# Single weight jobs of the mixers and the second block written as one 512-column and one 256-column matmul per k tile

## The chip, the cores and the metric

The kernel runs on one core of one Trainium2 chip. The metric is the device time of one execution in microseconds (us), as the median of several runs. The core has a matrix engine (PE, or TensorE, with its weight loads shown apart as PEld), two engines for elementwise work (ACT, or ScalarE, and DVE, or VectorE), a slower third (POOL, or GpSimd) and SP, which here only issues DMA transfers. Each engine works through its own instructions in a fixed order; they wait for one another by semaphores.

## What is computed

The reference is two stacked models on a sequence of 256 positions of width 2048, in fp32. The first has two layers, each of four mixers on one projection and a gated feed-forward part (5632 wide):

```python
for l in range(DEPTH):
    u = rms_norm(h, norm_pre_mix[l])
    p = (u @ w_in[l]).astype(jnp.float32)
    p_ret, p_hgrn, p_ml, p_rw = split_cols(p, GROUP_COLS)
    o_ret = retention_group(p_ret)
    o_hgrn = hgrn2_group(p_hgrn, lower_bounds[l], hgrn_norm_w[l])
    o_ml = mlstm_group(p_ml, ...)
    o_rw, v_first = rwkv7_group(p_rw, ...)
    mixed = jnp.concatenate([o_ret, o_hgrn, o_ml, o_rw], axis=-1) @ w_out[l]
    h = h + rms_norm(mixed, norm_post_mix[l])
    u = rms_norm(h, norm_pre_ffn[l])
    ffn = (jax.nn.silu(u @ w_ffn_gate[l]) * (u @ w_ffn_up[l])) @ w_ffn_down[l]
    h = h + rms_norm(ffn, norm_post_ffn[l])
```

The second ("block 2") is one layer of sparse attention and dilated attention on another such projection, merged and added to its input.

## The kernel before

**How a product is made.** All large products are weight streams: 512 KB of weights at a time come by a DMA of SP into a `raw` buffer (3 of them); `prep` (line 97) splits them into a high part `hi` (ACT's CAST, L108) and a low part `lo` (DVE's subtraction, L112), with 4 buffers of each; PE multiplies them with the activations, which are kept split in the same way, side by side in one tile of 512 columns: `x_hi` in columns 0 to 255, `x_lo` in 256 to 511. A product of fp32 accuracy is the sum hi·x_hi + hi·x_lo + lo·x_hi.

**Two kinds of streams.** `stream_a` (line 115) makes a block of 128 outputs, transposed, from 16 k tiles of 128 inputs, with the weights loaded into PE (128x128) and the activations streamed. A job is a tuple (weights, what to do at the end, a flag). With the flag True, a k tile takes three matmuls of 256 columns, all into the left half of a PSUM bank (L174 hi·x_hi, L175 hi·x_lo, L176 lo·x_hi): a *triple*. With False it takes one matmul of 512 columns, whose two halves are hi·x_hi and hi·x_lo (L178), and one of 256 columns for lo·x_hi into the left half (L179): a *pair*, and the two halves of the bank must be added afterwards. `half_sum` (L271) does so: ACT copies the right half out (L274), DVE adds the left half (L276). The feed-forward part and the merge at the end of block 2 use pairs, the mixers and block 2's other jobs triples. `stream_b` (line 213) makes 256x512 outputs with the activations loaded and the weights streamed, three 512-column matmuls to a step (L225, L226, L227), in two banks.

**Banks.** Streams take their banks from a pool of two (`sbank`, named `s` in the trace); the small products of the mixers use six others (`g`). A job of `stream_a` holds one `s` bank until its last reader is done, so the next job runs in the other; a `stream_b` takes both.

**The mixers.** `mixers` writes the code of a layer in a mixed order: 38 single jobs (`job_a`, L1342 is DVE's multiplication by the norm's factor at the job's end; `run_a`, `need`/`mix_job` call it) and 6 `run_b` of `stream_b`, and between them the small work of the four mixers, hundreds of matmuls of 32 to 128 columns with steps on ACT, DVE and POOL. The last third of a layer's mixers goes: RWKV7's output (`rw_out`, L1199 to L1234), the gates of mLSTM (`ml_gates`, L755 to L777), its values by `run_b(2)` (drained by ACT at L1512 into a tile `v`, with a memset of POOL ahead), then mLSTM's pairs. `v` and the gate tiles lie in memory that RWKV7's pool has given back, so the first to write them waits for the last steps of `rw_out`.

**Order.** The program is written with a scheduler that runs ahead of time: it estimates each instruction's duration, and within the priorities that the code sets (`K.first`, `issue_after`) fixes the order of each engine. So the order of the rows is a result, not written by hand, and another mix of instructions gives another order.

**Block 2.** 24 single jobs (`job`, L1888 is the ACT copy at a job's end) stand between the attention's work; 8 further jobs (those whose activations are `u`, with the flag 2) keep their triples in both kernels.

Of the kernel before, what the change touches and what calls it, by code (L numbers as in the profile page):

```python
# [13 lines left out]
OP = mybir.AluOpType  # L14
# [24 lines left out]
class Core:  # L39
# [228 lines left out]
            side = sides[i]  # L268
            self.stream_b(ws[i], orders[i] if orders else range(nk), lhs, done, None if side is None else [self.g(side), self.g(side)], i == 3, beside)

    def half_sum(self, bank):  # L271

        e0 = self.t(self.ev, [128, 256], "e0", 2)
        self.nc.scalar.copy(e0, bank[:, 256:512])  # L274
        e1 = self.t(self.ev, [128, 256], "e1", 2)
        self.nc.vector.tensor_tensor(e1, bank[:, 0:256], e0, op=OP.add)  # L276
        return e1

# [1046 lines left out]
def mixers(K, l, A, entry, dram, V):  # L1325

    nc, tc = K.nc, K.tc
    feed, late, rs, load = entry
    wa, wb = A[f"wina{l}"], A[f"winb{l}"]
    place = {n: i for i, n in enumerate(JOBS)}  # L1330
    outer, left, right = ExitStack(), ExitStack(), ExitStack()

    def pool(name, side, cx):
        return cx.enter_context(tc.tile_pool(name=f"{name}{l}", bufs=1, side=side, reuse_waits="tile"))

    def job_a(name, make):

        cell = []

        def done(bank):  # L1340
            dst, view = make()
            nc.vector.tensor_tensor(view, bank, rs(), op=OP.mult)  # L1342
            cell.append(dst)
        return (wa[place[name]], done, True), cell

    def run_a(name, make):
        job, cell = job_a(name, make)
        K.stream_a([job], K.uk, FULL)
        return cell[0]
# [7 lines left out]
    def padded(G, n, bufs=2):  # L1357
        def make():
            x = G.t([128, 256 + n], "x", bufs)
            nc.gpsimd.memset(x[:, 0:n], 0.0)  # L1360
            return x, x[:, n:256 + n]
        return make
# [12 lines left out]
    op = pool("o", "left", outer)  # L1375
# [8 lines left out]
    def mixed(x, i, name, bufs=1):  # L1384
        return R.shifted(x, w["mu"][:, i:i + 1], name, bufs)
# [7 lines left out]
    def mix_job(name):  # L1393
        (wt, done, _), cell = job_a(name, padded(R, 1))

        def both(bank):
            done(bank)
            i, to, bufs = where[name]
            got[name] = mixed(cell[0], i, to, bufs)
        return (wt, both, True)  # L1400

    def need(*names):
        for n in names:
            if n not in got:
                K.stream_a([mix_job(n)], K.uk, FULL, bank=K.g() if len(got) == 6 else None)
        return [got[n] for n in names]

    def begin(ph):
        load(ph)
        if ph[0] == 4:  # L1410
            w.update(columns(K, l, A))

    K.stream_a([mix_job(n) for n in HEADS], K.uk, FIRST if l else START, feed, late, load and begin, wa[0:4])
    rs.nat()
    w["wua"] = wua
# [57 lines left out]
    op = pool("o0", "right", right)  # L1473
# [26 lines left out]
    op = pool("o2", "left", left)  # L1500
# [110 lines left out]
class Ada:  # L1611
# [7 lines left out]
    def done(self):  # L1619

        K, nc = self.K, self.K.nc
        vec = K.t(K.base, [128, 80], "vec2")
        with K.tc.issue_after(K.last_hi.ins):
            nc.scalar.dma_start(vec, self.A["vec2"])
        nc.vector.tensor_tensor(self.cols, self.cols, vec[:, 0:48], op=OP.add)
        self.shift = self.cols[:, 0:16]
        self.scl = K.t(K.base, [128, 16], "scl")
        nc.vector.scalar_tensor_tensor(self.scl, self.cols[:, 16:32], 1.0, vec[:, 48:64], op0=OP.add, op1=OP.mult)
        self.post = K.t(K.base, [128, 16], "post")
        nc.vector.tensor_tensor(self.post, self.cols[:, 32:48], vec[:, 64:80], op=OP.mult)  # L1630
        self.kvb = K.t(K.base, [128, 8], "kvb")
        self.zero = K.t(K.base, [128, KT], "zero")
        nc.vector.memset(self.zero, 0.0)
# [193 lines left out]
def block2(K, A, mo, ada, prow):  # L1827

    nc, tc = K.nc, K.tc
    G = Groups(K, None, 2)  # L1830
    T = Attn(K, A)
    ja, jb = iter(range(200)), iter(range(10))
    wa, wb = A["win2a"], A["win2b"]
# [13 lines left out]
    with ExitStack() as cx:  # L1847
# [5 lines left out]
        feed, late, rs, _ = K.entry(scl, mo, lambda k: u1[:, k], keep=hs)  # L1853
# [29 lines left out]
    def job(name, bufs=1, p=None):  # L1883
        cell = []

        def done(bank):
            x = T.t([128, 256], name, bufs)
            nc.scalar.copy(x, bank)  # L1888
            cell.append(x)
        return (wa[next(ja)], done, True), cell  # L1890

    def run_a(name, bufs=1):
        j, cell = job(name, bufs)
        K.stream_a([j], K.uk, FULL)
        return cell[0]
# [259 lines left out]
```

## Time and profile before

| | us |
|---|---|
| median of 3 runs | 3503.91 (3499.05 to 3507.26) |
| profiled execution | 3503.24 |
| its span (first to last instruction) | 3501.4 |
| mixers, first and second layer | about 30 to 600, 1370 to 1940 |
| feed-forward parts | about 600 to 1345, 1940 to 2685 |
| block 2, its single jobs | about 2790 to 3040 |
| block 2, merge | about 3130 to 3490 |

| engine | busy in the whole span |
|---|---|
| PE | 3460.7 us (99%) |
| DVE | 2381.8 us (68%) |
| ACT | 1749.0 us (50%) |
| POOL | 492.8 us (14%) |

A row of the timeline gives the start, the duration, engine and line, operation, what is written from what, and in square brackets how long the engine had been idle and what it waited for. Matmuls overlap in the trace: their own durations are longer than the distance from one start to the next, and that distance is what a matmul takes from PE's time. The granted clock (PEclk) is a share of 2.4 GHz; 0.50 means 1.2 GHz.

### The profile page before, as it was taken

The page shows a single profiled execution, that of the slowest core. Times are in us where ns is not written, and L with a number is a line of the kernel's source. Part 1 is how long each engine was busy: PE and PEld are TensorE (multiplying, and loading weights), DVE is VectorE, ACT ScalarE, POOL GpSimd, SP SyncE. Part 2 cuts the span into 40 slices and gives each one's busy share as a digit, 9 for nine tenths or more (in the row PEclk, how much of TensorE's full clock was granted, in tenths as well). Part 3 has the DMA queues.
Part 4 walks back from the last instruction along what each step waited for, and adds up shares of the span by engine and source line. Part 5 has one row for each costly group of instructions (what it writes and reads, how often), then busy time and mean ns, then how long its engine had stood idle before and what let it go on. Part 6 is the DMA issues. An engine that isn't in the chain of part 4 may idle for free.

```text
span 3501.4 us, 58741 instructions
## 1 busy us (share of the span) xinstructions
PE 3460.7 (99%) x22403; PEld 2978.7 (85%) x22403; DVE 2381.8 (68%) x4330; ACT 1749.0 (50%) x2890; POOL 492.8 (14%) x686
## 2 busy tenths in 40 slices
PE   9999999999999999999999999999999999999998
PEld 8878888888888888888897888888888899988887
DVE  7776875777776546887785777776545766765554
ACT  5654544544444445655454544444345544554443
POOL 2122310211110001121320111111000112100000
PEclk9999999999999999999999999999999999999999
DMA  6334555666766665424456666666665545445555
GB/s 217 116 115 148 172 181 171 232 235 235 240 235 227 213 194 178 156 80 156 163 173 192 198 235 235 238 236 233 219 195 172 191 156 169 139 130 188 186 187 177
DMA packets 208554, 657.48 MB, mean 188 GB/s; under 512 B 24256, under 2 KB 27632, under 8 KB 208272
## 3 DMA queue, kind: packets, MB, share of 16 engines
q1 hardware_dynamic: 165952, 577.84, 50.6%
q10 hardware_dynamic: 42320, 75.89, 6.5%
q8 instruction: 176, 2.88, 0.3%
q14 instruction: 106, 0.87, 0.1%
HBM read 650.99 MB, written 2.65 MB: 187 GB/s over the span
## 4 chain that ended last, share of the span: by engine, by line
PE 95%; DVE 3%; ACT 1%; DMA 1%; issue 1%; POOL 0%; ACTq 0%; DVEq 0%; SPq 0%; POOLq 0%
PE s L178 23%; PE s L179 11%; PE s L225 8%; PE s L226 8%; PE s L227 8%; PE s L174 5%; PE s L175 5%; PE s L176 5%; PE g L225 4%; PE g L227 4%; PE g L226 4%; PE g L178 1%; PE g L175 1%; PE g L174 1%; PE g L176 1%
## 5 line engine op out<-in xcount | busy, mean ns | idle before, releaser
L112 DVE TENSOR_TENSOR lo<-raw,hi 128x1024 fp32r<-128x1024 f32 (+1 forms) x1089 | 1384.8, 1273 | 882.4 <-ACT hi L108 878.0
L108 ACT CAST hi<-raw 128x1024 fp32r<-128x1024 f32 (+1 forms) x1089 | 1139.5, 1049 | 1298.7 <-PE s L178 352.5
L178 PE MATMUL s<-uq,hi 128*128 128x512 f32 x3168 | 1111.4, 393 | 3.2 <-DVE e L276 3.2
L179 PE MATMUL s<-uq,lo 128*128 128x256 f32 x3168 | 884.2, 279 | 0.0
L178 PEld LDWEIGHTS s<-uq,hi 128*128 128x128 f32 x3168 | 593.6, 187 | 145.5 <-ACT hi L108 3.6
L179 PEld LDWEIGHTS s<-uq,lo 128*128 128x128 f32 x3168 | 593.7, 187 | 0.2
L174 PE MATMUL s<-uq,hi 128*128 128x256 f32 x1440 | 416.9, 290 | 5.2 <-ACT v L1512 2.5
L176 PE MATMUL s<-uq,lo 128*128 128x256 f32 x1440 | 416.0, 289 | 0.0
L175 PE MATMUL s<-uq,hi 128*128 128x256 f32 x1440 | 415.4, 288 | 0.0
L174 PEld LDWEIGHTS s<-uq,hi 128*128 128x128 f32 x1440 | 275.3, 191 | 14.3 <-issue 5.7
L175 PEld LDWEIGHTS s<-uq,hi 128*128 128x128 f32 x1440 | 275.1, 191 | 6.9 <-issue 6.1
L176 PEld LDWEIGHTS s<-uq,lo 128*128 128x128 f32 x1440 | 275.0, 191 | 6.8 <-issue 6.0
L226 PE MATMUL s<-lo,uq 128*128 128x512 f32 x672 | 269.4, 401 | 1.5 <-DVE lo L112 1.5
L227 PE MATMUL s<-hi,uq 128*128 128x512 f32 x672 | 267.8, 400 | 0.0
L225 PE MATMUL s<-hi,uq 128*128 128x512 f32 x672 | 266.5, 402 | 0.6 <-DVE k L1342 0.4
L444 POOL TENSOR_TENSOR gs<-e,R 128x256 f32<-128x256 f32 x88 | 77.8, 884 | 750.8 <-DVE e L276 412.9
L226 PEld LDWEIGHTS s<-lo,uq 128*128 128x128 f32 x672 | 127.4, 190 | 32.6 <-DVE lo L112 3.3
L225 PEld LDWEIGHTS s<-hi,uq 128*128 128x128 f32 x672 | 127.2, 189 | 32.0 <-issue 1.7
L227 PEld LDWEIGHTS s<-hi,uq 128*128 128x128 f32 x672 | 127.1, 189 | 30.0 <-issue 1.2
L225 PE MATMUL g<-hi,hid 128*128 128x512 f32 x352 | 139.2, 396 | 0.0
L226 PE MATMUL g<-lo,hid 128*128 128x512 f32 x352 | 139.2, 396 | 0.0
L227 PE MATMUL g<-hi,hid 128*128 128x512 f32 x352 | 139.2, 396 | 0.0
(639 smaller groups left out, 5311.2 us busy)
## 6 DMA issues: line engine op xcount, KB each, us to landing
raw<-in_wd_dram SPq DMA_DIRECT2D x176, 512.0 KB, 3.9
raw<-in_wg_dram SPq DMA_DIRECT2D x168, 512.0 KB, 4.1
raw<-in_wu_dram SPq DMA_DIRECT2D x168, 512.0 KB, 4.5
raw<-in_wina_dram SPq DMA_DIRECT2D x154, 512.0 KB, 3.8
raw<-in_win2a_dram SPq DMA_DIRECT2D x130, 512.0 KB, 3.6
raw<-in_winb_dram SPq DMA_DIRECT2D x96, 512.0 KB, 3.6
raw<-in_wout_dram SPq DMA_DIRECT2D x96, 512.0 KB, 3.9
aw<-in_wada_dram ACTq DMA_DIRECT2D x192, 256.0 KB, 4.4
```

The lines of the kernel that those rows point to most:

```text
L108: self.last_hi = nc.scalar.copy(hi[:, :n], raw[:, :n])
L112: self.last = nc.vector.tensor_tensor(lo[:, :n], raw[:, :n], hi[:, :n].bitcast(F32), op=OP.subtract)
L174: nc.tensor.matmul(banks[i][:, 0:n], wh, x[:, 0:n], start=first, stop=False)
L175: nc.tensor.matmul(banks[i][:, 0:n], wh, x[:, n:2 * n], start=False, stop=False)
L176: nc.tensor.matmul(banks[i][:, 0:n], wl, x[:, 0:n], start=False, stop=last)
L178: nc.tensor.matmul(banks[i], wh, x, start=first, stop=False)
L179: nc.tensor.matmul(banks[i][:, 0:256], wl, x[:, 0:256], start=False, stop=last)
L225: nc.tensor.matmul(banks[tt], xh, wh, start=(i + j == 0), stop=False)
L226: nc.tensor.matmul(banks[tt], xh, wl, start=False, stop=False)
L227: self.last_mm = nc.tensor.matmul(banks[tt], xl, wh, start=False, stop=(end and j == 1))
L444: nc.gpsimd.tensor_tensor(g, e, rget(), op=OP.mult)
```

## The change

```diff
-    def half_sum(self, bank):
+    def half_sum(self, bank, out=None):
         e0 = self.t(self.ev, [128, 256], "e0", 2)
         self.nc.scalar.copy(e0, bank[:, 256:512])
-        e1 = self.t(self.ev, [128, 256], "e1", 2)
+        e1 = self.t(self.ev, [128, 256], "e1", 2) if out is None else out
         self.nc.vector.tensor_tensor(e1, bank[:, 0:256], e0, op=OP.add)
         return e1
...
         def done(bank):
             dst, view = make()
-            nc.vector.tensor_tensor(view, bank, rs(), op=OP.mult)
+            nc.vector.tensor_tensor(view, K.half_sum(bank), rs(), op=OP.mult)
             cell.append(dst)
-        return (wa[place[name]], done, True), cell
+        return (wa[place[name]], done, False), cell
...
-        return (wt, both, True)
+        return (wt, both, False)
...
         def done(bank):
             x = T.t([128, 256], name, bufs)
-            nc.scalar.copy(x, bank)
+            K.half_sum(bank, x)
             cell.append(x)
-        return (wa[next(ja)], done, True), cell
+        return (wa[next(ja)], done, False), cell
```

The hunks stand, in this order, in `half_sum`, `job_a` and `mix_job` of the mixers, and block 2's `job`. It concerns 38 jobs in each of two layers and 24 in block 2: 100 jobs of 16 k tiles, 1600 triples that become pairs. PE's matmuls go from 20350 to 18750, with as many weight loads. A mixer job ends with ACT's copy (L274), DVE's addition (L276) and DVE's multiplication (L1342) instead of the multiplication alone, a job of block 2 with ACT's copy and DVE's addition instead of ACT's copy alone. The order that the scheduler fixes is another one. Three places of it follow; the number at the end of a name is one of the program's buffers.

**PE, first layer's mixers, RWKV7's and HGRN2's small work.** Before, three of its groups stand within some nine triples:

```order
L174 MATMUL s<-uq,hi 128x256
L1168 MATMUL g<-wW_779,wTT_909 64x128
L1102 MATMUL g<-ident,wT_1211 128x128
L1104 MATMUL g<-wLI,wT_1211 32x128
L942 MATMUL g<-hZ 32x32 x16
L1104 MATMUL g<-wLI,wT_1211 32x128
L1168 MATMUL g<-wW_779,wTT_909 64x128
L1104 MATMUL g<-wLI,wT_1211 32x128
L1168 MATMUL g<-wW_779,wTT_909 64x128
L1104 MATMUL g<-wLI,wT_1211 32x128
L1168 MATMUL g<-wW_779,wTT_909 64x128 x5
L175 MATMUL s<-uq,hi 128x256
```

After, a larger group stands between the two matmuls of one pair:

```order
L178 MATMUL s<-uq,hi 128x512
L1147 MATMUL g<-wT_719,wW_695 32x32 x8
L942 MATMUL g<-hZ 32x32 x48
L1074 MATMUL g<-wAR_1072,wKB 128x128 x8
L942 MATMUL g<-hZ 32x32 x32
L942 MATMUL g<-q,f 32x32 x16
L1154 MATMUL g<-wT_719,wQ 32x32 x8
L1162 MATMUL g<-wW_695 64x64 x8
L179 MATMUL s<-uq,lo 128x256
```

The triples are pairs, and the small work is cut into other groups: the stream is interrupted by small matmuls in 298 places where it was in 339 before.

**ACT, second layer, around the end of `run_b(2)`.** Before, the drain stands behind two casts and ahead of the rest of the gates' work (`md`, L793):

```order
L787 DMA md<-mm_91 128x768
L108 CAST hi<-raw 128x1024 [waits DMAHW0_49,PE_49]
L108 CAST hi<-raw 128x1024 [waits DMAHW1_49,PE_49]
L1512 ACTIVATE v<-s,Rn 128x8x64 [waits PE_49] x2
L108 CAST hi<-raw 128x1024 [waits DMAHW4_49,Activation_49]
```

After, it waits for DVE and POOL, and the gates' work stands behind it:

```order
L108 CAST hi<-raw 128x1024 [waits DMAHW7_49,PE_49]
L620 DMA c_mlstm<-in_c_mlstm_dram 128x640
L1372 DMA nw<-in_nat_dram 128x512
L1505 DMA gb<-in_gb_dram 8x2
L1512 ACTIVATE v<-s,Rn 128x8x64 [waits DVE_49,Pool_49]
L1512 ACTIVATE v<-s,Rn 128x8x64
L755 ACTIVATE mgf<-e_17809,gb 8x256 [waits DMAHW5_49]
```

What it waits for on DVE is the second L1233 of `rw_out` in this piece, which stands behind a subtraction (L112) of a later weight tile:

```order
L1232 TENSOR_TENSOR o_13260<-o_13260,ms 128x512 x2
L1233 TENSOR_TENSOR o_13260<-o_13260,wW_16946 128x512
L112 TENSOR_TENSOR lo<-raw,hi 128x1024
L1233 TENSOR_TENSOR o_13260<-o_13260,wW_16946 128x512
L1234 TENSOR_TENSOR o_13260<-o_13260,g 128x512 x2
L763 SCALAR_TENSOR_TENSOR mgf<-mgf,mge 8x256
```

`rw_out` moved back against the stream, so that its end falls together with the end of `run_b(2)`. The cast ahead of that L112 is the first CAST of the ACT piece, and it writes the buffer that the last matmul of `run_b(2)` reads.

**ACT, first layer, at the same place.** Before, the drain stands behind two of the L793:

```order
L793 ACTIVATE md<-md 128x384 [waits DMAHW7_49,DVE_49]
L793 ACTIVATE md<-md 128x384 [waits DVE_49]
L1512 ACTIVATE v<-s,Rn 128x8x64 [waits PE_49] x2
L108 CAST hi<-raw 128x1024 [waits DMAHW1_49,Activation_49]
L793 ACTIVATE md<-md 128x384 [waits DMAHW0_49,DVE_49]
```

After, it stands behind the gates' first steps, which need the small transfer `gb`:

```order
L1505 DMA gb<-in_gb_dram 8x2
L108 CAST hi<-raw 128x1024 [waits DMAHW0_49,DVE_49,PE_49]
L755 ACTIVATE mgf<-e_4587,gb 8x256 [waits DMAHW4_49]
L757 ACTIVATE mgi<-e_4587,gb 8x256
L759 ACTIVATE mge<-mgf 8x256 [waits Activation_49]
L310 ACT_TABLE_LOAD
L761 ACTIVATE mge<-mge 8x256 [waits Activation_49]
L108 CAST hi<-raw 128x1024 [waits DMAHW1_49,DVE_49,PE_49]
L762 ACTIVATE mge<-mge,cc 8x256 [waits Activation_49]
L1512 ACTIVATE v<-s,Rn 128x8x64 [waits DVE_49,PE_49]
L1512 ACTIVATE v<-s,Rn 128x8x64 [waits PE_49]
```

The gates moved from well before the end of `run_b(2)` to its end. In both layers PE has no small matmul to do there after the change: behind the last L227 comes the next job's first L178, with the next small group 22 and 26 pairs later, where before eight transposes (L634) stood between.

## Rows read from the trace of the kernel before

**Rows 1.** The page: busy time by engine, and the chain that ended last, by engine.

```profile
PE 3460.7 (99%) x22403; PEld 2978.7 (85%) x22403; DVE 2381.8 (68%) x4330; ACT 1749.0 (50%) x2890; POOL 492.8 (14%) x686
...
PE 95%; DVE 3%; ACT 1%; DMA 1%; issue 1%; POOL 0%; ACTq 0%; DVEq 0%; SPq 0%; POOLq 0%
```

**Rows 2.** A stretch, first layer's mixers: length, busy PE, PEld, DVE, ACT, POOL, clock, DMA.

```profile
30.00:600.00 570.00, 561.70 (x4669) 482.48 (x4668) 423.26 (x890) 290.47 (x523) 115.78 (x180) 0.99 0.49 157
```

**Rows 3.** Line L174, matmuls with `uq`: count, ns min/median/max, first and last start.

```profile
L174 PE MATMUL s<-uq,hi x1440: 274/282/682, 33.7 to 3035.3; 128*128 128x256 f32 x180
...
L174 PE MATMUL g<-uq,hi x160: 274/282/579, 5.6 to 1391.7; 128*128 128x256 f32 x160
```

**Rows 4.** Timeline of PE in a mixer job: first and eleventh triple's start.

```profile
303.15 0.28 PE L174 MATMUL s<-uq,hi 128*128 128x256 f32 x1
...
306.75 0.28 PE L174 MATMUL s<-uq,hi 128*128 128x256 f32 x1
```

**Rows 5.** Timeline of PE in the feed-forward part: first and 46th pair's start.

```profile
1000.01 0.39 PE L178 MATMUL s<-uq,hi 128*128 128x512 f32 x1
1000.25 0.28 PE L179 MATMUL s<-uq,lo 128*128 128x256 f32 x1
...
1015.77 0.39 PE L178 MATMUL s<-uq,hi 128*128 128x512 f32 x1
```

**Rows 6.** Timeline of PE just behind a group of small matmuls in the stream.

```profile
302.58 0.38 PE L176 MATMUL s<-uq,lo 128*128 128x256 f32 x1
...
302.80 0.28 PE L174 MATMUL s<-uq,hi 128*128 128x256 f32 x1
```

**Rows 7.** Lines L1342, L274, L276 (ns min/median/max); last, waits for L276: us, times.

```profile
L1342 DVE TENSOR_TENSOR x<-s,R x34: 409/418/428, 48.9 to 1794.4; 128x256 f32<-128x256 f32 x34
...
L274 ACT COPY e<-s x230: 354/367/373, 636.4 to 3409.1; 128x256 f32<-128x256 f32 x115
...
L276 DVE TENSOR_TENSOR e<-s,e x230: 409/418/423, 643.0 to 3410.4; 128x256 f32<-128x256 f32 x115
...
  DVE e L276: 6.6, 19
```

**Rows 8.** Waits of PE, first layer's mixers: us in total, times, longest.

```profile
PE s L225 <- DVE k L1342: 0.4, 1, 0.4
```

**Rows 9.** Timeline at the end of a mixer job: its last matmul, and DVE's step.

```profile
305.20 0.28 PE L176 MATMUL s<-uq,lo 128*128 128x256 f32 x1
...
305.51 0.42 DVE L1342 TENSOR_TENSOR q<-s,R 128x256 f32<-128x256 f32 x1 [1.13 <-PE s L176]
```

**Rows 10.** Timeline, first layer: PE's next job behind `run_b(2)`.

```profile
398.93 0.58 PE L174 MATMUL s<-uq,hi 128*128 128x256 f32 x1 [2.54 <-ACT v L1512]
```

**Rows 11.** Timeline of ACT, first layer: first and last gate step; then a DMA's landing time.

```profile
376.94 0.51 ACT L755 ACTIVATE mgf<-e,gb 8x256 f32<-8x256 f32 x1 [1.88 <-DVE e L1508]
...
381.95 0.50 ACT L762 ACTIVATE mge<-mge,cc 8x256 f32<-8x256 f32 x1
...
gain<-in_gain_dram ACTq DMA_DIRECT2D x16, 256.0 KB, 4.1
```

**Rows 12.** Timeline, second layer: the drain of `run_b(2)` and PE's next job.

```profile
1738.74 1.39 ACT L1512 ACTIVATE v<-s,Rn 128x512 f32<-128x512 f32 x2 [1.42 <-PE s L227]
...
1740.04 0.36 PE L174 MATMUL s<-uq,hi 128*128 128x256 f32 x1
```

**Rows 13.** Lines L108, L112, L1233: ns min/median/max of one.

```profile
L108 ACT CAST hi<-raw x1089: 617/1051/1073, 4.5 to 3480.1; 128x1024 fp32r<-128x1024 f32 x181, 128x512 fp32r<-128x512 f32 x1
...
L112 DVE TENSOR_TENSOR lo<-raw,hi x1089: 693/1226/2289, 5.2 to 3481.2; 128x1024 fp32r<-128x1024 f32 x181, 128x512 fp32r<-128x512 f32 x1
...
L1233 DVE TENSOR_TENSOR o<-o,wW x4: 895/1221/1226, 366.4 to 1711.4; 128x512 f32<-128x512 f32 x4
```

**Rows 14.** Stretches at half clock behind a wait of PE; columns as in rows 2.

```profile
398.90:402.30 3.40, 3.37 (x16) 3.37 (x16) 3.40 (x6) 3.31 (x6) 0.00 (x0) 0.50 0.10 34
...
2788.30:2795.10 6.80, 6.18 (x28) 5.32 (x26) 2.82 (x3) 2.15 (x4) 0.00 (x0) 0.50 0.92 295
```

## The prediction, made before the changed kernel was run

> **What bounds the kernel now.** I read the page first: engine shares, then the chain of work that ended last. PE is busy 99% of the span, and 95% of the chain is PE [rows 1]; DVE has 68% and ACT 50%. So every nanosecond that PE's row of instructions gets shorter counts in full, and every wait of PE that is added counts in full too; work on other engines counts only where PE then waits for it. The stretch of the first layer's mixers says the same of the place: 561.70 of 570 us PE, 423.26 DVE, 290.47 ACT, clock 0.99 [rows 2]. The third view is the timeline of PE alone, where the distance from one start to the next is what a matmul costs.
>
> **What it saves on PE.** The line's own rows give 1440 + 160 = 1600 triples with `uq` [rows 3]; all become pairs. Ten triples take 306.75 − 303.15 = 3.60 us, 0.3600 each [rows 4]. Forty-five pairs take 1015.77 − 1000.01 = 15.76 us, 0.3502 each [rows 5]. Both stream the same 768 columns; the pair has one matmul fewer. The difference is 9.8 ns, and 1600 × 9.8 ns = 15.7 us. Both rows are read to 0.01 us, so one triple is uncertain by 1 ns: 14 to 17 us.
>
> The first stream matmul behind a group of small ones starts later: from the L176 behind the group to the next L174 it is 0.22 us, where 0.12 is the rule inside a triple (a third of 0.360) [rows 4, 6]. The order has 298 such places for 339 before, 41 fewer: 41 × 0.10 = 4.1 us. Since a group that is split or joined costs between nothing and 0.2 us, I bound this by 0 and 8.
>
> The Trainium skill, page "TensorE: Matmul & The Clock Gate", section "Back-to-back issue gap", puts a warm matmul's distance at its columns by 2.4 GHz and some 2.5 ns more. The rows disagree: they have 9.8 ns for the matmul that goes. By the page 1600 × 2.5 ns = 4 us would be saved, an estimate, and the sum below would be 3496 + 11.7 = 3508.
>
> **What it adds on ACT and DVE.** A mixer job's end was one DVE step of 0.418 us (L1342). Now ACT's copy, 0.367 us, and DVE's addition, 0.418 us, stand ahead of it [rows 7]. That is 38 × 0.418 = 15.9 us more DVE and 13.9 us more ACT in a layer's mixers, so DVE goes from 423 to 439 of 570 us [rows 2]: room enough. A job of block 2 has DVE's 0.418 more, 24 times 10 us. From one job to the next this is hidden: the next job runs in the other bank for 16 × 0.350 = 5.6 us, and the bank is free again after about 1.1. In the feed-forward parts, where the same additions end the jobs, PE has waited for them 6.6 us in 19 cases out of 240 [rows 7]: the cover holds but for changes of stream.
>
> *Into a `run_b`.* There both banks are wanted. At the end of a job the last matmul starts at 305.20 and L1342 runs from 305.51 to 305.93, so the bank is free 0.73 us after that start [rows 9]. The `run_b` that follows asks for it after one 256-column and three 512-column matmuls, 0.12 + 3 × 0.233 = 0.82 us (0.233 is two thirds of a pair) [rows 4, 5]. So far it just fits; one case had a wait of 0.4 [rows 8]. With copy and addition the bank is free after 0.31 + 0.37 + 0.03 + 0.42 = 1.13 us, 0.3 too late where both engines are idle; a CAST of 1.05 us that ACT has begun [rows 13] makes it up to 1.4. Four such places a layer and two in block 2 are 10. I take 0.4 each, as in rows 8 and near 6.6 / 19 = 0.35 in rows 7: +4.0 us, bounds 0 (small matmuls stand between) and 14.
>
> **What the new order moves.** *Second layer, the end of `run_b(2)`.* Before, ACT drained it at once (1738.74), and PE's next job began at 1740.04 with no wait [rows 12]. Now L1512 waits for the second L1233, that for an L112, and that for a CAST which may only write when the last matmul of `run_b(2)` has read the buffer. Queued behind: the gates' whole chain on ACT; PE waits, since both banks are held and no small matmul stands there. One after the other: CAST 1.05, L112 1.23, L1233 1.22 (0.90 at the fastest) [rows 13], first L1512 0.70 (half of 1.39) [rows 12], less some 0.1 of overlap: **+4.1 us**, bounds 3 and 5.
>
> *First layer, the same place.* PE already waits 2.54 us for L1512 [rows 10]. Now L1512 stands behind L755 to L762, which need `gb`, issued behind an ACT copy that waits for PE 34 stream matmuls, 34 × 0.233 = 7.9 us, ahead of the end of `run_b(2)`. From there: copy 0.37 and three issues about 1, landing 4.1 as a transfer of ACT's queue has it, gate steps 382.45 − 376.94 = 5.5 (with a CAST between), L1512 0.70 [rows 7, 11, 12]: 11.7, less 7.9 is 3.8, and some 0.2 for signals: 4.0 instead of 2.5, **+1.5 us**. `gb` is tiny but stands behind two larger transfers, so the landing may take 2 to 7 us: bounds −2 and +4.
>
> *The clock behind a wait.* Behind the 2.54 us wait the granted clock was 0.50 from 398.9 for 3.4 us, and from 2788.3, behind another, for 6.8 us [rows 10, 14]. At 1.2 GHz PE does half the work, so such a stretch costs 1.7 or 3.4 us. The first layer has its stretch already. The new wait of 4.1 us in the second layer is longer than the one at 398.9, so I count one: **+2.5 us**, the middle, bounds 0 and 3.4.
>
> The small groups in the mixers stand elsewhere against the stream, 10 to 55 k tiles later. Each has a chain between PE, ACT and DVE in front of it. Nothing in the profile says that the new places fit worse or better, so this stands at 0 in the sum and carries two of the rivals.
>
> **The sum.** −15.7 − 4.1 + 4.0 + 4.1 + 1.5 + 2.5 = −7.7 us. The profiled execution took 3503.24 us, 0.67 below the median, 1.8 above its span; 3495.5 by it, 3496.2 from the median. I say **3496**. With the terms' bounds taken together as independent it is 3488 to 3504.
>
> **The rivals.**
> *One: the full gain.* Waits for drains fall beside small matmuls, and the new order has as many waits as the old. Then only the first two terms count: 3503.2 − 19.8 = 3483. For it speaks that PE's share leaves few waits [rows 1]; against it that L1512's wait in the second layer has nothing beside it.
> *Two: the gain is eaten.* Three more waits of some 2.5 us, as in rows 10, at the places to which the small groups have moved: 3496 + 7.5 = 3503. For it speaks that the order was another for all of the mixers' work and DVE's 74% leaves small work queued.
> *Three, the other side: waits that bring down the clock.* The chains of small work run PE to DVE to PE; the end of a job now puts two DVE steps and one ACT step, 1.2 us, in front of them, where one of 0.42 stood. Where PE then stands still as long as in rows 10, half clock follows: 2.5 + 1.7 to 3.4, about 5 us each [rows 10, 14]. From one to two more of these the gain is gone (7.7 / 5), from three on the kernel is slower; four give 3496 + 20 = 3516. Against it: the whole mixers' stretch of 570 us has only 8 us without PE [rows 2].
> *Four: a matmul less saves only a quarter of this.* Rows 5 read L178 to L179 as 0.24, twice the 0.12 of rows 4; taken so, the matmul that goes costs hardly anything, and the 9.8 ns belong to the feed-forward's surroundings. A quarter of 15.7 us is 3.9: 3496 + 11.8 = 3508. The 15.76 us of 45 pairs [rows 5] speak against it. The page cited above has about this size.
> That the change does not do what it says can be left out: the order has pairs in all 1600 places.
>
> **How the numbers follow.** Forecast 0.40, one 0.17, two 0.20, three 0.17, four 0.04, and 0.02 for something still slower. A measurement of this kernel can tell about 0.2%, 7 us, from no change: faster is below 3497, slower above 3511. Of the forecast's 0.40, with a sum on the edge, I put 0.28 below 3497 and 0.12 above. Faster 0.28 + 0.17 = 0.45; the same 0.12 + 0.20 + 0.04 = 0.36; slower 0.17 + 0.02 = 0.19. The range runs from a little under the full gain to just over rival three's four events, 3480 to 3517; the forecast's own is 3488 to 3504.
>
> **What would show it.** In the profile after, L178 and L179 have 1600 more each, with some 0.350 us from pair to pair in the mixers; 0.357 or more is rival four. A wait of PE's L178 for ACT's L1512 of about 4 us in each layer, half clock behind the second; no such wait means rival one. In the waits of PE, L225 for DVE's L276 some ten times, 0.3 to 0.5 each. DVE some 16 us busier in a layer's mixers, ACT 14. A mean clock of 0.99 in the first layer's mixers, as before [rows 2], speaks against rival three, 0.98 or less for it. The forecast is wrong if new waits of over 2 us stand at small matmuls (two and three), or if the first layer's L1512 waits for something other than the gates.

## The result: slower by 0.6%

The changed kernel takes 3521.72 us (median of 6 runs, 3514.69 to 3532.13), the kernel before 3504.35 beside it (6 runs). The ratio is 1.0059 with a 95% interval of 1.0048 to 1.0070. The forecast was 3496, faster; the range of 3480 to 3517 did not hold it.

The profiled execution after took 3520.54 us, its span is 3518.8. The page's busy times and its chain, to be laid beside [rows 1]:

```profile
PE 3458.8 (98%) x20803; PEld 2894.0 (82%) x20803; DVE 2415.7 (69%) x4430; ACT 1772.7 (50%) x2966; POOL 464.0 (13%) x686
...
PE 91%; DVE 5%; DMA 1%; issue 1%; ACT 1%; POOL 0%; ACTq 0%; SPq 0%; DVEq 0%; POOLq 0%
```

PE has 1600 matmuls fewer and is busy for 1.9 us less only; its share of the chain fell from 95 to 91%, DVE's rose from 3 to 5%.

**The pairs do what was said.** Timeline of PE after, in a mixer job: the first and the 46th pair's start.

```profile
41.61 0.39 PE L178 MATMUL s<-uq,hi 128*128 128x512 f32 x1
...
57.36 0.39 PE L178 MATMUL s<-uq,hi 128*128 128x512 f32 x1
```

45 pairs in 15.75 us are 0.350 each, as in [rows 5], against 0.360 for a triple [rows 4].

**PE waits more.** The longest of PE's waits after, over the whole span (total, times, longest):

```profile
PE s L178 <- ACT v L1512: 8.8, 2, 5.4
PE g L369 <- DMA h<-in_x_dram: 6.3, 2, 3.5
PE s L178 <- DVE e L276: 3.6, 2, 1.9
PE g L1751 <- DVE kr L1740: 3.1, 2, 2.1
PE g L178 <- DVE uq L337: 2.5, 3, 0.8
PE g L942 <- issue: 2.4, 3, 1.8
PE s L178 <- ACT v L1368: 2.4, 2, 2.2
PE s L225 <- DVE e L276: 2.2, 2, 1.7
```

All entries of this view sum to 47.7 us; those of the same view of the kernel before to 28.9. That is 18.8 us more, about what pairs and fewer interruptions save (15.7 + 4.1).

**And the clock does the rest.** Each run comes with its mean granted clock. If PE did half the work at half clock, a run would have lost (1 − clock) × time. That is an upper bound: in the changed kernel a pair at half clock took 1751.62 − 1750.98 = 0.64 us (two starts of L178) where it takes 0.350 else, so it lost 0.45 of its time and not half. The 82 runs of the kernel before in the experiments below have a mean of 3503.1 us and 20.0 us lost by this measure; the six of the changed kernel 3523.3 and 39.4. So of 20.2 us more, up to 19.4 are clock, by the pair's 0.45 about 17.6, and the rest is small. The spread of the changed kernel's own runs is of the same kind: 3514.69 at 0.991, 3532.13 at 0.986; 17.4 us between them, and 0.005 × 3520 = 17.6.

Where it lies shows in stretches of the dense small work, RWKV7's and HGRN2's, first and second layer (columns as in [rows 2]). The kernel before:

```profile
120.00:230.00 110.00, 106.71 (x1663) 88.69 (x1664) 91.39 (x288) 60.77 (x163) 29.85 (x54) 0.95 0.25 80
...
1460.00:1580.00 120.00, 118.41 (x1718) 98.23 (x1717) 97.65 (x295) 65.86 (x171) 29.95 (x54) 0.94 0.30 97
```

The changed kernel:

```profile
120.00:230.00 110.00, 104.47 (x1427) 82.00 (x1427) 90.94 (x269) 59.29 (x156) 27.71 (x52) 0.91 0.26 88
...
1460.00:1580.00 120.00, 113.15 (x1522) 88.21 (x1521) 96.04 (x282) 64.89 (x165) 29.95 (x52) 0.90 0.30 99
```

Two things are to be seen. PE is without work for 5.5 and 6.9 us where it was 3.3 and 1.6, and the clock fell from 0.95 and 0.94 to 0.91 and 0.90. And DVE was already busy 83 and 81% here before the change, not the 74% of the whole stretch [rows 2].

### The profile page after: what moved, and what is told of

The parts are those of the page before. It is cut to its first block, busy times and chain, and to the rows that moved or that the text cites. A ratio compares the mean times of both kernels' runs of the same rounds, so it can differ in the third digit from the quotient of the medians.

```text
span 3518.8 us, 55734 instructions
## 1 busy us (share of the span) xinstructions
PE 3458.8 (98%) x20803; PEld 2894.0 (82%) x20803; DVE 2415.7 (69%) x4430; ACT 1772.7 (50%) x2966; POOL 464.0 (13%) x686
## 4 chain that ended last, share of the span: by engine, by line
PE 91%; DVE 5%; DMA 1%; issue 1%; ACT 1%; POOL 0%; ACTq 0%; SPq 0%; DVEq 0%; POOLq 0%
PE s L178 31%; PE s L179 16%; PE s L225 7%; PE s L227 7%; PE s L226 7%; PE g L225 4%; PE g L226 4%; PE g L227 4%; PE g L178 2%; DVE lo L112 1%; PE g L179 1%; PE g L1751 1%; PE g L369 0%; PE g L1192 0%; ACT hi L108 0%
## 5 line engine op out<-in xcount | busy, mean ns | idle before, releaser
L112 DVE TENSOR_TENSOR lo<-raw,hi 128x1024 fp32r<-128x1024 f32 (+1 forms) x1089 | 1382.9, 1271 | 881.5 <-ACT hi L108 877.0
L108 ACT CAST hi<-raw 128x1024 fp32r<-128x1024 f32 (+1 forms) x1089 | 1140.5, 1049 | 1293.2 <-PE s L178 481.6
L178 PE MATMUL s<-uq,hi 128*128 128x512 f32 x4608 | 1643.1, 397 | 16.0 <-ACT v L1512 8.8
L178 PEld LDWEIGHTS s<-uq,hi 128*128 128x128 f32 x4608 | 870.4, 189 | 227.6 <-ACT v L1512 9.7
L227 PE MATMUL s<-hi,uq 128*128 128x512 f32 x672 | 269.8, 403 | 0.0
L225 PE MATMUL s<-hi,uq 128*128 128x512 f32 x672 | 266.4, 404 | 2.4 <-DVE e L276 2.2
L444 POOL TENSOR_TENSOR gs<-e,R 128x256 f32<-128x256 f32 x88 | 67.8, 771 | 755.6 <-DVE e L276 418.2
L225 PEld LDWEIGHTS s<-hi,uq 128*128 128x128 f32 x672 | 127.8, 190 | 34.4 <-DVE e L276 3.2
L227 PEld LDWEIGHTS s<-hi,uq 128*128 128x128 f32 x672 | 127.9, 190 | 30.5 <-issue 1.2
L227 PE MATMUL g<-hi,hid 128*128 128x512 f32 x352 | 139.2, 396 | 0.0
L225 PE MATMUL s<-hi,hid 128*128 128x512 f32 x352 | 139.2, 396 | 0.0
L226 PE MATMUL s<-lo,hid 128*128 128x512 f32 x352 | 139.2, 396 | 0.0
L227 PE MATMUL s<-hi,hid 128*128 128x512 f32 x352 | 139.2, 395 | 0.0
L225 PE MATMUL g<-hi,hid 128*128 128x512 f32 x352 | 139.2, 395 | 0.0
L276 DVE TENSOR_TENSOR e<-s,e 128x256 f32<-128x256 f32 x296 | 123.7, 418 | 1.5 <-ACT e L274 1.2
L450 POOL TENSOR_TENSOR e<-e,R 128x256 f32<-128x256 f32 x88 | 69.8, 793 | 384.0 <-DVE e L276 382.5
L178 PE MATMUL g<-uq,hi 128*128 128x512 f32 x320 | 117.4, 407 | 2.5 <-DVE uq L337 2.5
```

Of the source, the lines that this page charges most:

```text
L108: self.last_hi = nc.scalar.copy(hi[:, :n], raw[:, :n])
L112: self.last = nc.vector.tensor_tensor(lo[:, :n], raw[:, :n], hi[:, :n].bitcast(F32), op=OP.subtract)
L178: nc.tensor.matmul(banks[i], wh, x, start=first, stop=False)
L225: nc.tensor.matmul(banks[tt], xh, wh, start=(i + j == 0), stop=False)
L226: nc.tensor.matmul(banks[tt], xh, wl, start=False, stop=False)
L227: self.last_mm = nc.tensor.matmul(banks[tt], xl, wh, start=False, stop=(end and j == 1))
```

## The experiments

The clock's part is given for each as the mean of (1 − clock) × time over its runs, an upper bound as said above, and *rest* is the mean time less that: 3503.1, 20.0 and 3483.1 for the kernel before, 3523.3, 39.4 and 3484.0 for the changed one. By the traces the scheduler made an order of its own in all of these runs but e_mv, whose order is nearly that of the changed kernel; so, but for the two runs that change the order on purpose, the others change more than the one thing that their edit names.

| run | what it is | median us | ratio to before (95%) | lost at half clock | rest |
|---|---|---|---|---|---|
| e_l1 | second layer's mixers alone | 3516.09 | 1.0038 (1.0023 to 1.0053) | 26.4 | 3489.2 |
| e_l0b2 | first layer's and block 2 alone | 3511.50 | 1.0026 (1.0016 to 1.0036) | 28.9 | 3482.8 |
| e_noepi | pairs without the additions | 3501.32 | 0.9993 (0.9983 to 1.0002) | 25.9 | 3474.5 |
| e_epi | additions without the pairs | 3538.77 | 1.0097 (1.0061 to 1.0133) | 37.2 | 3498.5 |
| e_ord | before, another order | 3505.31 | 1.0008 (0.9999 to 1.0017) | 23.3 | 3481.6 |
| e_ord2 | changed, another order | 3526.06 | 1.0073 (1.0060 to 1.0086) | 46.4 | 3479.7 |
| e_mv | changed, L1512's wait shortened | 3524.45 | 1.0068 (1.0055 to 1.0080) | 40.9 | 3484.1 |
| e_fill | changed, bunches filled | 3606.95 | 1.0297 (1.0283 to 1.0311) | 80.3 | 3527.0 |
| e_pool | changed, product on POOL | 3510.87 | 1.0021 (1.0010 to 1.0032) | 28.1 | 3482.8 |
| e_load | before, with the load alone | 3511.21 | 1.0024 (1.0013 to 1.0036) | 25.2 | 3486.7 |
| e_lat | before, with a longer end alone | 3504.71 | 1.0008 (0.9999 to 1.0017) | 16.1 | 3489.9 |
| b_part | 768 of 1600 pairs | 3506.28 | 1.0007 (0.9998 to 1.0015) | 24.9 | 3479.4 |
| b_qk | 512 of 1600 pairs | 3503.68 | 1.0004 (0.9995 to 1.0013) | 19.1 | 3485.2 |
| b_last | 768 pairs, another order | 3503.93 | 1.0002 (0.9993 to 1.0011) | 21.3 | 3483.3 |

### Which place: e_l1 and e_l0b2

In the changed kernel's one trace nearly all of the loss lay in the second layer: the first layer's feed-forward part began 0.8 us later than before, the second layer's 17.9 us later. Was it that layer's order?

```diff
-        return (wa[place[name]], done, False), cell
+        return (wa[place[name]], done, not (l == 1)), cell
```

and for e_l0b2 `(l == 0)`, with the same condition on `half_sum`; block 2 as before in e_l1, changed in e_l0b2.

> Only the 38 mixer jobs of the second layer become pairs (608 of the 1600 triples); the first layer and block 2 stay as before, and so does their order. Theory 1 (the order of the second layer's small work, with its waits of PE and the half clock behind them, made the change slow): in the changed kernel the stretch from the start of the second layer's mixers to their end is some 16 us longer, so nearly all of the loss stays, 3515 to 3522 us, with 30 us or more at half clock in that layer. Theory 2 (the additions at the jobs' ends delay PE, equally at each job): 38 of 100 jobs, so +6 to +7 us, about 3510. Theory 3 (pairs leave PE too lightly used, so that the clock falls wherever they stand): also by share of jobs, about 3510.

> Only the first layer's mixers and block 2 become pairs (992 of 1600); the second layer's mixers keep triples, and nearly keep their order. Theory 1: the loss goes; in the changed kernel the first layer's stretch was 0.8 us longer and block 2 some 1.5 us shorter, so 3500 to 3506, the same as before. Theory 2: 62 of 100 jobs, +10 us, about 3514. Theory 3: +10 us as well.

Measured were +0.38% and +0.26%, 13.6 and 9.0 us on the medians. Theory 1's time for e_l1 came (3516.09 in 3515 to 3522), but e_l0b2 was to lose nothing by it and lost 9.0, so the second layer's order is not the one place. Theory 2 has e_l0b2 (about 3514, measured 3511.50) and misses e_l1, which was to lose 6 to 7. The two parts together make 22.6 us, where the whole change's medians are 17.4 apart, and they do not go by the number of jobs: 38 jobs cost 13.6 us, the other 62 cost 9.0. One trace had misled: in e_l0b2's, the second layer's mixers keep triples, and yet from the first POOL step (L444) of the first layer's feed-forward part to that of the second's it is 6.6 us longer than before.

### Which half of the change: e_noepi and e_epi

```diff
-            nc.vector.tensor_tensor(view, K.half_sum(bank), rs(), op=OP.mult)
+            nc.vector.tensor_tensor(view, bank[:, 0:256], rs(), op=OP.mult)
```

is e_noepi on the changed kernel (a plain ACT copy in block 2). e_epi is on the kernel before:

```diff
-            nc.vector.tensor_tensor(view, bank, rs(), op=OP.mult)
+            nc.vector.tensor_tensor(view, half_max(K, bank), rs(), op=OP.mult)
...
+def half_max(K, bank, out=None):
+    e0 = K.t(K.ev, [128, 256], "e0", 2)
+    K.nc.scalar.copy(e0, bank)
+    e1 = K.t(K.ev, [128, 256], "e1", 2) if out is None else out
+    K.nc.vector.tensor_tensor(e1, bank, e0, op=OP.max)
+    return e1
```

> All 1600 triples become pairs, but the jobs end as before: one DVE or ACT step that reads the left half of the bank alone, so the product of the weights' high part with the activations' low part is left out of the result. PE's work is that of the changed kernel, ACT's and DVE's that of the kernel before; the order is a third one. Theory 1: time is set by the order, the jobs' ends matter only through it; the small work stands 12 to 30 k tiles later than before, between the two kernels, so some of the waits and of the half clock go: 3495 to 3515. Theory 2: the gain of 15 to 20 us comes out in full, 3484 to 3490. Theory 3: still slow, 3515 or more.

> All triples stay; the jobs end with ACT's copy of the bank, a DVE step (the maximum of bank and copy, which is the bank itself) and, in the mixers, the multiplication. PE's work is that of the kernel before, ACT's and DVE's that of the changed kernel; the order is a fourth one, with the small work some 8 k tiles off. Theory 1: 3500 to 3512, by what waits and half clock this order happens to have. Theory 2: the whole loss without the gain on PE: 3504 + 17 + 15 = about 3536. Theory 3: as before, 3504.

The additions alone cost 0.97%, the pairs alone change nothing that can be told (0.9983 to 1.0002). So the loss comes with the ends of the jobs, as theory 2 had it for e_epi (about 3536). Theory 3, the pairs themselves, is out: all 1600 are in e_noepi. But theory 2's 3484 to 3490 for e_noepi did not come either (3501.32 lies in theory 1's 3495 to 3515): the rest fell by 8.6 us, and the clock took some 6 back. All waits of PE in e_noepi sum to 41.3 us, 12.4 more than before; the first lines show where they are:

```profile
PE g L369 <- DMA h<-in_x_dram: 6.0, 2, 3.4
PE g L684 <- DVE mgf L665: 5.0, 3, 2.7
PE s L178 <- DVE e L276: 3.9, 2, 2.0
PE g L942 <- issue: 3.1, 2, 2.3
```

The stream gets shorter, the chains of the small work do not, and PE waits at other places (L684 and L942 are the mixers' small matmuls; L369, at the very start, waits for the model's input). In e_epi the second layer's dense stretch ran at a clock of 0.80:

```profile
1460.00:1580.00 120.00, 113.00 (x1359) 90.88 (x1357) 88.39 (x256) 59.52 (x153) 25.69 (x47) 0.80 0.26 85
...
1512.00:1535.90 23.90, 23.90 (x199) 16.37 (x202) 8.95 (x26) 7.07 (x19) 3.35 (x9) 0.50 0.14 44
```

The second line is one piece of it, 23.9 us at half clock, with PE busy in all of it; a wait of 1.4 us stands in the 8 us ahead of it. This kernel has triples in the mixers, so pairs are not needed for the half clock.

### Only the order: e_ord and e_ord2

```diff
-        with K.first(1000):
+        with K.first(300):
             H.hg_pair(p, q, lf[:, p], k[:, p], v, outs[1])
```

on the kernel before (e_ord) and on the changed one (e_ord2).

> The kernel before, with one number changed: the priority offset of HGRN2's small work is 300 in place of 1000. Every instruction is that of the kernel before, only the order differs (groups of small work stand up to 49 k tiles elsewhere in the mixers). Theory 1 (where the small work lands in PE's row decides, by waits of PE and by half clock behind stretches without stream matmuls): 4 to 14 us slower than before, 3507 to 3517, with more waits and more half clock in the mixers alone. Theory 2 (the additions at the jobs' ends themselves delay PE): no difference, 3500 to 3505.

> The changed kernel, with the same one number changed to 300. Every instruction is that of the changed kernel, only the order differs. Theory 1: another time than 3522, by over 4 us, 3508 to 3532, with the second layer's stretch most different, since its groups stand 20 to 40 k tiles nearer to where they were before. Theory 2: 3522 within 3.

On the kernel before theory 1 missed: it moved by 2.7 us, with an interval that holds no change, though groups stood up to 49 k tiles elsewhere, and 3505.31 is at the upper end of theory 2's range. On the changed one nothing is decided: 3526.06 is 4.3 us over 3521.72, which by the letter is theory 1's "over 4 us", but the two intervals overlap. Within e_ord2 a half is worth noting: lost at half clock 46.4 in place of 39.4, and the rest 4.3 less. Where the small work lands trades waits against clock; this one shift of it moved the sum little.

### One named wait: e_mv

```diff
-    nw = bcast(M, 3, "nw")
+    mv = M.t([128, 2, 8, 65], "v")
     gb = M.t([8, 2], "gb")
...
-    mv = M.t([128, 2, 8, 65], "v")
...
-    M.ml_out(outs[2], mt, nw)
+    M.ml_out(outs[2], mt, bcast(M, 3, "nw"))
```

> The changed kernel, with mLSTM's tile for its values asked for ahead of the others of its pool, and the weights of its norm loaded where they are used, so that the drain of the second layer's third 512-column stream no longer writes memory that RWKV7's output step still reads. The order of PE's matmuls stays. Theory 1: that wait of PE falls from 5.4 to some 2 us (the CAST and the drain itself remain ahead), and the half clock at 1747 with it or not: 3 to 7 us faster than the changed kernel, 3515 to 3519; the rest of the loss stays. If the half clock is set by the bunches of small matmuls alone, 3 us only.

The wait went as meant:

```profile
PE s L178 <- DVE e L276: 4.9, 5, 1.7
PE s L178 <- ACT v L1512: 3.8, 2, 2.0
PE g L942 <- issue: 3.8, 3, 2.3
```

8.8 us became 3.8, and the time did not follow: 3524.45, the interval overlaps that of the change. The clock lost 40.9 and the rest is 3484.1, as in the changed kernel. 5 us of a wait were taken away, others (L276 and L942 above) grew by 2.7, and all waits of PE sum to 47.6 us, as in the changed kernel (47.7). So the longest wait was not the loss; no other was tried singly.

### What lowers the clock: e_fill

```diff
-                        n = x * 64 + tt * 32
+                        n = x * 64 + tt * 32; [nc.tensor.matmul(g2[h][:, 384:512], K.mean_r, K.mean_r, start=True, stop=True) for _ in range(4 if tt + j == 0 else 0)]
```

> The changed kernel with 384 further matmuls of 128x128 by 128 columns, four in front of each 16 small ones of HGRN2's levels, into columns of the bank that nothing reads; they only keep the matrix engine occupied inside the bunches of small work, and cost some 0.06 to 0.13 us each by the eight-matmul rows of L634, 23 to 50 us in all. Theory 1 with the clock set by the bunches: the share at half clock goes down though the kernel does more, from a mean clock of 0.988 to 0.992 or more, and the time to 3530 to 3555. If the half clock comes from somewhere else (the stream's pairs, the waits alone): clock 0.988 or lower, 3545 to 3575.

Both expectations missed the time by far: 3607 us. Of the two, the second had the clock's side (0.988 or lower, measured 0.978). Against the changed kernel the rest grew by 43.0 us and the clock's part by 40.9. The stretch of the first layer's dense work, and a piece in it:

```profile
120.00:230.00 110.00, 110.00 (x1151) 89.22 (x1149) 69.92 (x201) 45.50 (x121) 19.54 (x39) 0.78 0.21 69
144.60:192.40 47.80, 47.80 (x549) 39.16 (x543) 24.91 (x85) 9.72 (x31) 5.91 (x14) 0.50 0.06 19
```

PE has no idle time in the 110 us, and the clock fell from 0.91 to 0.78, with 47.8 us at half clock on end. The timeline of PE inside that piece:

```profile
150.06 0.44 PE L942 MATMUL g<-hZ 64*32 64x32 f32 x16
150.43 1.11 PE L940 MATMUL g<-mean 128*128 128x128 f32 x4
151.47 0.44 PE L942 MATMUL g<-hZ 64*32 64x32 f32 x16
```

The added matmuls make the bunches longer: from 140.9 to 190.1 us only five of the stream's wide matmuls stand in PE's row. So here the clock fell inside bunches of matmuls of 32 to 128 columns with no wait of PE that the profile shows, neither in the piece nor in the 24.6 us ahead of it, and it stayed down for longer than anywhere in the changed kernel (17.1 us). "Busy" is not full work, though: at full clock four fillers take 141.90 − 141.31 = 0.59 us (the same timeline), 0.15 for 128 columns each, where 256 columns of the stream take 0.12 [rows 4]. What this run can't say is what wide fillers would have done.

The Trainium skill, page "TensorE: Matmul & The Clock Gate", section "HAM oscillation — how this bites in real kernels", puts the throttling down to gaps in which PE idles. The waits of [rows 10, 14] agree. The second line of the stretch above, 47.80 us busy of 47.80 at 0.50, does not, and here the measurement decides.

### DVE's share of it: e_pool

```diff
-            nc.vector.tensor_tensor(view, K.half_sum(bank), rs(), op=OP.mult)
+            nc.gpsimd.tensor_tensor(view, K.half_sum(bank, view), rs(), op=OP.mult)
```

> The changed kernel with the multiplication at a mixer job's end moved from DVE to POOL, and the sum written straight into the job's own tile: the ends of the jobs put one DVE step in front of the small work instead of two, and POOL's slower one behind it. All 1600 pairs stay. If it is DVE's queue at the ends that delays the small work: 8 to 18 us faster than the changed kernel, 3503 to 3515. If it is the length of the end itself (copy, sum, product, one after the other): no faster, 3520 to 3530.

3510.87 is inside the first expectation. The end of a job is not shorter, a DVE step has gone to a slower engine, and 11.3 of the 39.4 us at half clock are gone, with a rest that differs by 1.2. That is more than half of the loss. The order that came out is another one too, so it is not DVE's step alone that differs. And DVE's share of the dense stretch is not smaller for it: in e_pool DVE is busy for 101.55 of the 120 us of the second layer's, against 96.04 in the changed kernel.

### Load or length: e_load and e_lat

Both on the kernel before:

```diff
             nc.vector.tensor_tensor(view, bank, rs(), op=OP.mult)
-            cell.append(dst)
+            dead(K, view); cell.append(dst)
...
+def dead(K, x):
+    e0 = K.t(K.ev, [128, 256], "e0", 2)
+    K.nc.scalar.copy(e0, x)
+    e1 = K.t(K.ev, [128, 256], "e1", 2)
+    K.nc.vector.tensor_tensor(e1, x, e0, op=OP.add)
```

(e_load), and for e_lat `through(K, bank)`, a copy by ACT, in the place of `bank`.

> The kernel before with, behind the end of each of the 76 mixer jobs, ACT's copy and DVE's addition of 256 columns on the job's finished tile, and behind each of the 24 jobs of block 2 one DVE copy; nothing reads what they write. Triples, and the chain from a job's last matmul to the small work, are those of before; ACT and DVE have the changed kernel's load. If the load of DVE and ACT is what delays the small work: 8 to 20 us slower than before, 3511 to 3523. If the longer chain at the job's end does it: 3500 to 3506.

> The kernel before with the mixer jobs' multiplication reading a copy that ACT makes of the bank, instead of the bank: the chain is 0.37 us longer and passes through ACT's queue with its casts of 1.05 us; DVE's work is that of before. Triples as before. If the longer chain through ACT delays the small work: 3511 to 3523. If DVE's load does: 3500 to 3506.

The load costs 0.24%, 7.7 us on the medians, though nothing waits for its results; 3511.21 is at the lower end of the range for the load. The longer end through ACT's queue costs nothing that can be told. (The order is another one in both: by the traces small matmuls stand up to 27 k tiles elsewhere in e_load and 41 in e_lat. Against its being the order alone speaks e_ord, 2.7 us.) The dense stretches of e_load:

```profile
120.00:230.00 110.00, 105.53 (x1620) 88.47 (x1618) 90.69 (x285) 57.64 (x157) 29.06 (x54) 0.89 0.23 74
...
1460.00:1580.00 120.00, 116.10 (x1685) 96.69 (x1684) 105.36 (x307) 70.38 (x173) 30.38 (x54) 0.94 0.32 103
```

DVE is 88% busy in the second layer's, where it was 81%, and PE has 3.9 us without work there for 1.6; in the first layer's the clock is 0.89 for 0.95. Load and length together make e_epi's 36 us, far more than 7.7 and 1.2. What fails to add is the clock's part above all: against the kernel before, the rest is up by 3.6 in e_load, 6.8 in e_lat and 15.4 in e_epi; the clock's part by 5.2, −3.9 and 17.2. In e_epi a job also holds its bank until ACT's copy and DVE's step behind it are done, longer than in e_load and e_lat, and PE waits for that twice at L225, 5.6 us in all. Why the clock's parts do not add, these runs do not settle.

### Fewer pairs: b_part, b_qk, b_last

With conditions on the job's name in place of the changed flag: the four first jobs, RWKV7's k, and q and k of retention and mLSTM (b_part, and b_last with `K.first(50)` for RWKV7), or the q and k of those two alone (b_qk).

> Pairs only for the four first jobs of a layer, RWKV7's k, retention's and mLSTM's q and k (48 of 76 mixer jobs, 768 of 1600 triples); the others, and block 2, as before. The first layer's small work still stands up to 43 k tiles off, the second's 3 to 23. Theory 1: 768 x 9.8 ns = 7.5 us saved, with the second layer's waits and half clock near those of before: 3490 to 3500. Theory 2: 48 of 100 jobs of the loss, 9 us slower than before, 3511.

> Pairs only for retention's and mLSTM's q and k (32 of 76 mixer jobs, 512 of 1600 triples, 5.0 us), whose small work has few small matmuls in a chain; RWKV7's and HGRN2's jobs and block 2 as before, the sum written straight into the job's tile. The order stays as before in most of the mixers, up to 31 k tiles off in the last third. Theory 1: the gain comes out but for waits at the ends of streams, 3495 to 3502. If each job with an addition at its end costs something wherever it stands (32 of 100 jobs of some 20 us): 3506 to 3510.

> Pairs only for the four first jobs of a layer, RWKV7's k, retention's and mLSTM's q and k (768 of 1600 triples, 7.5 us), the sum written straight into the job's own tile, and RWKV7's small work at priority offset 50 in place of 100; block 2 as before. If what decides is where the small work lands, an order that happens to fit gives 3492 to 3500; if each addition costs by its load, 3504 to 3510.

None differs from the kernel before, and each time lies between the ranges of its two theories. The 5.0 and 7.5 us on PE did not come out, in two selections of jobs, the larger of them in two orders; the best of them, b_last, has 1.0002. A version that beats the kernel before was not found.

## Why the prediction was wrong

**The terms that were worked out nearly held.** PE's saving of 19.8 us is there by the sum: 18.8 us more waits leave the rest as it was. The pair is 0.350 us in the mixers too, so rival four is out. L1512 made PE wait in the second layer:

```profile
1749.43 1.27 ACT L1512 ACTIVATE v<-s,Rn 128x512 f32<-128x512 f32 x2 [3.61 <-DVE o L1233]
...
1750.17 0.79 PE L178 MATMUL s<-uq,hi 128*128 128x512 f32 x1 [5.43 <-ACT v L1512]
```

5.4 us where the sum had 4.1 (rows of `rw_out`'s own were late too), and behind it half clock, as said. In the first layer it was 3.4 us for 4.0:

```profile
397.71 0.50 PE L178 MATMUL s<-uq,hi 128*128 128x512 f32 x1 [3.39 <-ACT v L1512]
```

L225 waited for L276 twice with 2.2 us where ten times 0.4 were expected. These waits came out at 8.8 − 2.5 + 2.2 − 0.4 = 8.1 us more, for 9.6 in the sum. Two readings were off without bearing on this: rows 7 have 230 additions and not 240, and the terms' bounds, taken as independent, reach 3507 and not 3504.

**The step that failed** is the sentence that the small groups' new places stand "at 0 in the sum", and ahead of it the words "room enough" for DVE. The 0 had no row behind it, only that the profile said nothing; what came is 18.8 − 8.1 = 10.7 us of waits at other places than the sum's three, and the half clock of the next paragraph. "Room enough" rests on an average: 423 to 439 us of 570 [rows 2]. The small work is not spread over 570 us. In the two stretches where it is dense DVE was busy for 91.39 of 110 and 97.65 of 120 us before the change. That the ends of the jobs bring the loss is shown: e_epi has it with triples, e_noepi is without it with pairs. Less work on PE turned into waits (e_noepi), more load on ACT and DVE cost time though nothing read its results (e_load), and a DVE step less gave over half back (e_pool). That it goes by DVE's queue is argued from these and not shown: in the changed kernel's second dense stretch PE's waits name ACT for 3.2 us, issue for 2.1 and DVE for 1.3, and DVE's share there does not follow the loss (e_pool). The page's 99% for PE hid that it may be kept in step by others.

**The term that was mis-sized** is the clock: +2.5 us in the sum, up to +19.4 measured. The sum counted one stretch behind one wait, and half the work at half clock where pairs lose 0.45 of their time. The changed kernel's trace has ten pieces at half clock ahead of its last 10 us; in the 8 us ahead of each PE was without work for 0.6 to 3.4 us, and in most of them bunches of small matmuls stand there too, so that this trace does not tell the two apart. Two of its pieces, the longest, behind a bunch with a wait of 1.0 us (L720, for ACT), and the one behind L1512's wait:

```profile
1531.90:1549.00 17.10, 17.10 (x99) 11.26 (x101) 8.39 (x24) 6.71 (x19) 1.45 (x3) 0.50 0.16 54
1747.00:1753.80 6.80, 3.63 (x11) 3.15 (x12) 3.62 (x6) 4.01 (x7) 0.19 (x3) 0.50 0.60 200
```

The kernel before had a piece behind a bunch without a wait. The first line is the time between the piece before it and this one, PE busy in all of it, mostly with small matmuls:

```profile
1491.10:1498.00 6.90, 6.90 (x64) 5.77 (x62) 4.14 (x11) 2.74 (x9) 1.83 (x5) 0.99 0.25 76
1498.00:1504.80 6.80, 6.80 (x62) 6.21 (x65) 6.24 (x23) 2.46 (x6) 1.51 (x3) 0.50 0.00 1
```

So a row that would have warned of it was there.

**Rival three came nearest.** It had the side, the place (DVE steps in front of the small chains, half clock behind), and 3516 for four events; measured are 3522. Its chance of 0.17 was too low, and its argument against, only 8 us without PE in the whole stretch [rows 2], was again the average. Its sign came too, a clock of 0.98 in the first layer's mixers. It named waits as long as that of rows 10 as the trigger. New waits of over 2 us at small matmuls came once (L1751, 2.1 us), and the half clock also came without a wait (e_fill, and the two lines above).

**What stays open:** by which path the ends of the jobs bring on waits and half clock; why load and longer end together cost some 36 us and apart 9; and how much of the changed kernel's loss is the order that the scheduler chose, since no run has the pairs in the order of before.

## What to carry to other kernels

An engine at 99% need not be the only bound where chains of small work run between it and others: look at the waits, the clock and the other engines' shares in the stretch where that work is dense, not over the stage. Here a saving on the first engine came back as waits, and steps added to the others cost time even where nothing read what they wrote. A term for which the profile shows nothing is not 0; it is unknown, and belongs in the range. And compare kernels with small matmuls by several runs and by the clock's part of each, since one trace's account by stages moves by as much as the effect.

## What the runs showed of the hardware

The granted clock fell to 0.50 with PE busy throughout as the profile counts it: 47.8 us on end in e_fill, nearly all of it bunches of matmuls of 32 to 128 columns. A pair took 0.64 us at half clock for 0.350, not twice as long. The time of one kernel varies with the clock from run to run, 3520.98 us at a mean clock of 0.994 to 3544.15 at 0.987 in e_epi: 23 us, where 0.007 × 3540 is 25.
